# Scales of two attentions spread over partitions by transposes on TensorE instead of through a row in DRAM, and two matmul groups reordered by height

## Chip, core and metric

The kernel runs on one core of one Trainium2 chip. The metric is the device time of one execution in microseconds, the median of three runs.

## The reference, cut to what matters

The reference is one transformer block followed by a second block of two layers, on a sequence of 1024 tokens of width 1024, in float32. The first block mixes tokens by a chunked gated linear attention (4 heads) and by a causal attention with low-rank projections (MLA, 8 heads with values of 64 channels); a cross attention to 256 memory tokens and a feed-forward part with a short convolution follow. The second block has an even layer (a state-space scan beside a long convolution) and an odd layer, a differential attention of 8 heads with values of 128 channels:

```
MLA:   p = softmax(sc);  o = p @ v                        (8 heads, 64 channels)
odd:   wts = softmax(sc_0) - lam * softmax(sc_1);  o = wts @ v     (8 heads, 128 channels)
       o = rmsnorm(o, subln_w) * (1 - lam_init);  o = o * silu(gate);  out = x + o @ w_out
GLA:   o_intra + o_inter = (q k^T, masked) v + q S;   S <- decay * S + k^T v   (chunks of 64)
even:  decay = exp(where(tril, cs_l - cs_s, -inf)) for each head and chunk
```

In both attentions each query's output has one factor that is known only after its scores: the reciprocal of the softmax sum in the MLA attention, the reciprocal root of the mean square in the odd one.

## The kernel before

A sequence of stages, each with its own tile pools, goes over 8 tiles of 128 tokens. Matmuls work on split operands, a high and a low part, with three matmuls for each product (`mm3`, lines 263 to 265). PSUM has four buffers of 512 columns (`pa`) and two of 1024 (`pb`). The framework lays the instructions of each engine in one order when the program is built, by priority in the order of the code, with waits on semaphores between engines; `later` shifts the priority.

The frame of both attentions is `attend`. It walks over steps, each a head and a pair of query tiles `t0`, in the order 6, 4, 2, 0 (`ORDER`; the first MLA head the other way round). In a step it lays the scores of the next step, the transposes of this step's probabilities (`trans2`, line 773), the products with the values, and, through `pop`, some independent work from a queue: output projections, gate projections. A step ends with `finish`, which may return a function; that is called at the end of the next step, and what it returns again one step later. Four query tiles make a group `g` (0 or 1), two groups a head.

The outputs are held transposed: channels on partitions, tokens along the columns. The factors lie with tokens on partitions, one column for each tile. To multiply, the factors must stand along the columns on every partition:

- In the odd attention (`odd_attn`), `finish` makes `H.y`. `sums`, a step later, adds up the squares on TensorE and, with the second pair of a group, takes the root (`root`, lines 178 to 182: ten short VectorE instructions). It then writes the four columns as a row to DRAM (line 1633) and reads the row back to all 128 partitions (line 1635), both from SyncE's queue. `scale`, one step later again, multiplies on GpSimd (line 1617). Head 7's group 0 doesn't take this way: it is scaled at the output. When both groups of a head are scaled, `split_y` makes the high part on ScalarE (line 1679) and the low part on GpSimd (line 1680), and the output projections can use them.
- In the MLA attention (`mla`), two heads share a tile: 64 channels each. `norm` takes the reciprocal of four columns for each head (line 926), writes a row (line 928) and reads it to 64 partitions (line 931). After the odd head of a pair, `scale` multiplies on GpSimd (line 919), and the split into high and low follows on ScalarE and GpSimd (lines 920, 921). Heads 6 and 7 take another way for the first four tiles (`direct`).

Two other places are touched. In `gla`, `step` makes for each of four heads one matmul over 128 rows (line 624) and two over 64 rows (line 626) into one PSUM tile; each call of 128 columns stands as two instructions in the profile. In `even`, each of 4 heads in 8 turns takes one matmul of a selector column over 64 rows of `csT` (line 1291) and one of a mask over 128 rows (line 1292).

Of the kernel before, what the change touches and what calls it, by code (L numbers as in the profile page):

```python
# [19 lines left out]
P = 128  # L20
# [14 lines left out]
class Kern:  # L35
# [64 lines left out]
    def setup(self):  # L100
# [24 lines left out]
        self.sel = self.cpool_const([64, 16], F32R)  # L125
        nc.vector.tensor_tensor(self.sel, self.ident[:64, 0:16], self.ident[:64, 32:48], op=ALU.add)
# [447 lines left out]
    def gla(self, qT, ki, kt, E, vt, sg):  # L574
# [28 lines left out]
        def step(t):  # L603
# [16 lines left out]
            for hd in range(4):  # L620
                j, hh = hd // 2, hd % 2
                r = slice(hh * 64, hh * 64 + 64)
                ol = slice(hh * 512 + j * P, hh * 512 + j * P + P)
                mm(po[:, ol], at[t][:, hh * 2 + j], vt[t][:, hd * P:(hd + 1) * P], start=True, stop=False)
                for c in range(2):
                    mm(po[c * 64:(c + 1) * 64, ol], qT[j][r, t * P + c * 64:t * P + c * 64 + 64], S_in[c][j][r, :],
                       start=False, stop=True)
# [204 lines left out]
    def mla(self, h, qT, kT, v, side):  # L832
        nc, a = self.nc, self.a
        mm = nc.tensor.matmul
        pair, vhl, sums, rbs, raw = {}, {}, {}, {}, {}
# [19 lines left out]
        def scores(st, q):  # L855
# [14 lines left out]
            if hd not in sums:  # L870
                sums[hd] = self.small(8, tag="rsm", bufs=3)
            nm, rs = self.small(1, tag="nm", bufs=6), sums[hd][:, t:t + 1]
# [17 lines left out]
        def finish(step, po):  # L890
# [26 lines left out]
            def scale():  # L917
                gc = slice(g * 512, g * 512 + 512)
                nc.gpsimd.tensor_tensor(o, o, rbs[g], op=ALU.mult)
                nc.scalar.copy(oh[:, gc], o)  # L920
                nc.gpsimd.tensor_tensor(ol[:, gc], o, oh[:, gc].bitcast(F32), op=ALU.subtract)
                done(range(g * 4, g * 4 + 4))

            def norm():
                sg = sums[hd][:, g * 4:g * 4 + 4]
                nc.vector.reciprocal(sg, sg)
                row = self.dram.tile([4, P], F32, name="row1", tag="row1", bufs=4)
                nc.sync.dma_start(out=row.rearrange("t p -> p t"), in_=sg)
                if hd % 2 == 0:
                    rbs[g] = self.slot("rb", [P, 512])  # L930
                nc.sync.dma_start(out=rbs[g][r], in_=row.rearrange("t p -> (t p)").partition_broadcast(64))
                return scale if hd % 2 else None

            return norm
# [183 lines left out]
    def even(self, X, usum, rs, spill, zsp, ysp):  # L1118
# [72 lines left out]
        for g in range(4):  # L1191
# [52 lines left out]
            if g == 0:  # L1244
                csT = self.sb.tile([64, S], F32R, name="csT", tag="csT", bufs=1)
# [3 lines left out]
                nc.vector.tensor_scalar(csT, self.ident[:64, 0:1].to_broadcast([64, S]), 0.0, None, op0=ALU.mult)  # L1249
# [31 lines left out]
            for i in range(2):  # L1281
# [6 lines left out]
                for e in range(4):  # L1288
                    hd = 4 * g + e
                    ps = self.psum()  # L1290
                    mm(ps, self.sel[:, hd:hd + 1].to_broadcast([64, P]), csT[:, i * 512:(i + 1) * 512], start=True, stop=False)
# [220 lines left out]
    def odd_attn(self, X, h3, out, qs, ks, vs, gs):  # L1512
# [21 lines left out]
        def start(hd):  # L1534
# [12 lines left out]
            H.y, H.rb, H.yhl = None, {}, {}  # L1547
# [57 lines left out]
        def finish(st, po):  # L1605
# [8 lines left out]

            def scale():
                gc = slice(g * 512, g * 512 + 512)
                nc.gpsimd.tensor_tensor(H.y[:, gc], H.y[:, gc], H.rb[g], op=ALU.mult)
                H.scaled += 1

            def sums():  # L1620
# [6 lines left out]
                ts = self.last(t0)  # L1627
                if ts:
                    c = slice(ts[0], ts[0] + 4)
                    self.root(H.rstd[:, c], H.ss[:, c], self.small(4))  # L1630
                    if hd < 7 or g:
                        row = self.dram.tile([4, P], F32, name="row", tag="row", bufs=4)
                        nc.sync.dma_start(out=row.rearrange("t p -> p t"), in_=H.rstd[:, c])
                        H.rb[g] = self.slot("rb", [P, 512])
                        nc.sync.dma_start(out=H.rb[g], in_=row.rearrange("t p -> (t p)").partition_broadcast(P))
# [115 lines left out]
def body(tc, a, out, h_in=None, stages="ABCDE"):  # L1751
    with ExitStack() as ctx:
# [69 lines left out]
        if "E" in stages:  # L1822
# [13 lines left out]
            XO.enter_context(K.pool("oa", v=4, vu=2, vr=2, sg=2, pt=4, y=4, rb=2, gt=3, tmp=4))  # L1836
# [25 lines left out]
```

## Time and profile before

| | |
|---|---|
| median of 3 runs | 3262.02 us (3260.43 to 3266.59) |
| profiled execution | 3269.77 us; span 3267.8 us |
| mean granted clock of TensorE | 0.956 |
| linear attention, steps | about 220 to 282 us |
| MLA attention | about 385 to 625 us |
| even layer | about 1540 to 2290 us |
| odd attention | about 2780 to 3268 us |

Times in the profile are microseconds from the start of the span. PE is TensorE, PEld its loads of weights, DVE VectorE, ACT ScalarE, POOL GpSimd, SP SyncE. Busy time of an engine counts its instructions, not its waits. PEclk is the clock that TensorE was granted, as a share of full speed. A row of the windows view gives the stretch, its length, the busy time and count of instructions of PE, PEld, DVE, ACT and POOL, then PEclk, the share of time in which the DMA engines moved data, and GB/s. In a row of waits, the engine and line ahead of the arrow waited for what stands behind it.

### The profile page before, as it was taken

How to read it: one execution, taken by the hardware profiler on the slowest of the kernel's cores; microseconds unless marked ns; L12 is line 12 of the kernel's file. 1: busy time of each engine (PE TensorE's matmuls, PEld its weight loads, DVE VectorE, ACT ScalarE, POOL GpSimd, SP SyncE). 2: the span in 40 equal slices, each digit the busy share in tenths (PEclk: the TensorE clock that was granted, in tenths of full speed). 3: DMA queues.
4: the chain of work that ended last, by engine and by line, in shares of the span. 5: the costliest groups of instructions: out<-in, count | busy, mean ns of one | idle time of the engine just before them, and what ended most of it. 6: DMA issues, size and time to landing. Idle time of an engine off the chain costs nothing.

```text
span 3267.8 us, 38496 instructions
## 1 busy us (share of the span) xinstructions
PE 3020.2 (92%) x14638; PEld 2447.1 (75%) x14646; DVE 1930.5 (59%) x3114; ACT 1129.9 (35%) x2090; POOL 868.7 (27%) x776
## 2 busy tenths in 40 slices
PE   8999888889999999999999999999999999996777
PEld 7777666677788888888878777777777888784665
DVE  4324766765443334333898979785885550684555
ACT  4421554634311211121432323232334331553443
POOL 2111611112212221221134242434512220223434
PEclk9988989999999999999999999999999999997878
DMA  3011101110211111111211111123323562545321
GB/s 114 26 46 50 38 17 17 43 46 20 78 39 52 52 52 39 52 52 54 79 49 50 55 55 50 55 62 124 151 71 111 147 203 82 143 122 159 94 55 65
DMA packets 186156, 234.25 MB, mean 72 GB/s; under 512 B 31069, under 2 KB 121717, under 8 KB 185973
## 3 DMA queue, kind: packets, MB, share of 16 engines
q1 hardware_dynamic: 166901, 202.44, 20.9%
q10 hardware_dynamic: 15616, 16.78, 1.6%
q0 software_dynamic: 3456, 12.58, 1.0%
q8 instruction: 115, 1.88, 0.3%
q14 instruction: 68, 0.56, 0.1%
HBM read 181.37 MB, written 50.39 MB: 71 GB/s over the span
## 4 chain that ended last, share of the span: by engine, by line
PE 61%; DVE 14%; DMA 9%; issue 6%; POOL 4%; ACT 3%; SPq 0%; POOLq 0%; DVEq 0%; ACTq 0%
PE pa_t L263 9%; PE pa_t L264 9%; PE pa_t L265 9%; PE pb_t L265 8%; PE pb_t L264 8%; PE pb_t L263 8%; DMA row<-rsy_t 3%; DVE acc_t L1143 3%; DMA rb_t<-row 2%; PE pa_t L773 1%; PE pb_t L868 1%; DVE wl_t L202 1%; PE pa_t L887 1%; DVE h_t L290 1%; POOL wl_t L202 1%
## 5 line engine op out<-in xcount | busy, mean ns | idle before, releaser
L202 POOL TENSOR_TENSOR wl_t<-wr_t,wh_t 128x349 fp32r<-128x349 f32 (+2 forms) x221 | 294.9, 1337 | 1250.4 <-ACT wh_t L197 1208.7
L263 PE MATMUL pb_t<-x_t,wh_t 128*128 128x512 f32 x1312 | 518.5, 396 | 2.0 <-ACT wh_t L197 0.9
L265 PE MATMUL pb_t<-x_t,wl_t 128*128 128x512 f32 x1312 | 515.7, 393 | 0.9 <-DVE wl_t L202 0.9
L264 PE MATMUL pb_t<-x_t,wh_t 128*128 128x512 f32 x1280 | 505.3, 395 | 0.1
L197 ACT CAST wh_t<-wr_t 128x1024 fp32r<-128x1024 f32 (+2 forms) x221 | 217.4, 993 | 552.8 <-PE pb_t L264 256.2
L202 DVE TENSOR_TENSOR wl_t<-wr_t,wh_t 128x675 fp32r<-128x675 f32 (+1 forms) x195 | 207.8, 1070 | 305.4 <-ACT wh_t L197 304.9
L263 PE MATMUL pa_t<-wh_t,x_t 128*128 128x512 f32 (+3 forms) x1024 | 374.3, 366 | 2.6 <-ACT wh_t L197 0.8
L264 PE MATMUL pa_t<-wl_t,x_t 128*128 128x512 f32 (+3 forms) x1024 | 371.3, 363 | 0.5 <-DVE wl_t L202 0.3
L1143 DVE SCALAR_TENSOR_TENSOR acc_t<-u_t,c,acc_t 128x1024 f32<-128x1024 f32 x240 | 339.3, 1416 | 2.9
L290 DVE TENSOR_TENSOR h_t<-h_t,pa_t 128x512 f32<-128x512 f32 x336 | 226.5, 685 | 150.6 <-PE pa_t L265 148.7
L263 PEld LDWEIGHTS pb_t<-x_t,wh_t 128*128 128x128 f32 x1312 | 247.4, 189 | 57.1 <-ACT wh_t L197 1.8
L265 PEld LDWEIGHTS pb_t<-x_t,wl_t 128*128 128x128 f32 x1312 | 247.3, 188 | 55.6 <-DVE wl_t L202 2.1
L264 PEld LDWEIGHTS pb_t<-x_t,wh_t 128*128 128x128 f32 x1280 | 241.4, 189 | 52.9 <-DVE x_t L212 1.0
L265 PE MATMUL pa_t<-wh_t,x_t 128*128 128x512 f32 (+3 forms) x640 | 221.3, 346 | 0.0
L263 PEld LDWEIGHTS pa_t<-wh_t,x_t 128*128 128x128 f32 x1024 | 192.4, 188 | 33.7 <-ACT wh_t L197 2.0
L265 PE MATMUL pa_t<-wh_t,xl_t 128*128 128x512 f32 x512 | 205.6, 402 | 11.6 <-POOL xl_t L1680 11.6
L264 PEld LDWEIGHTS pa_t<-wl_t,x_t 128*128 128x128 f32 x1024 | 192.5, 188 | 30.9 <-DVE wl_t L202 2.1
L209 DVE TENSOR_TENSOR pt_t<-pa_t,pt_t 128x512 fp32r<-128x512 f32 (+2 forms) x240 | 120.0, 508 | 99.0 <-ACT pt_t L208 97.4
L263 PE MATMUL pa_t<-wh_t,g_t 128*128 128x512 f32 x384 | 150.2, 391 | 3.2 <-DVE h_t L290 1.4
L264 PE MATMUL pa_t<-wl_t,g_t 128*128 128x512 f32 x384 | 149.5, 389 | 0.0
L265 PE MATMUL pa_t<-wh_t,g_t 128*128 128x512 f32 x352 | 136.8, 389 | 1.1 <-POOL g_t L340 1.1
L208 ACT CAST pt_t<-pa_t 128x512 fp32r<-128x512 f32 (+2 forms) x240 | 105.5, 443 | 78.1 <-PE pa_t L773 49.5
(501 smaller groups left out, 5983.8 us busy)
## 6 DMA issues: line engine op xcount, KB each, us to landing
wr_t<-in_a_w_in SPq DMA_DIRECT2D x46, 512.0 KB
wr_t<-in_c_w_in SPq DMA_DIRECT2D x26, 512.0 KB
wr_t<-in_ffn_w_gate SPq DMA_DIRECT2D x22, 512.0 KB
wr_t<-in_ffn_w_up SPq DMA_DIRECT2D x22, 512.0 KB
wr_t<-in_ffn_w_down SPq DMA_DIRECT2D x22, 512.0 KB
h_t<-in_x SPq DMA_DIRECT2D x16, 512.0 KB
wr_t<-in_a_w_out SPq DMA_DIRECT2D x16, 512.0 KB
lo_t<-ks SPq DMA_DIRECT2D x64, 128.0 KB
```

The costliest lines, as they stand in the source:

```text
L197: nc.scalar.copy(hi, raw)
L202: e.tensor_tensor(*[x[:, c] for x in f], op=ALU.subtract)
L208: nc.scalar.copy(hi, src)
L209: nc.vector.tensor_tensor(lo, src, hi.bitcast(F32), op=ALU.subtract)
L263: mm(out, lh, rh, start=st, stop=False)
L264: mm(out, lh, rl, start=False, stop=False)
L265: mm(out, ll, rh, start=False, stop=en)
L290: self.nc.vector.tensor_tensor(h[t][:, c], h[t][:, c], ps, op=ALU.add)
L773: self.nc.tensor.transpose(pt[:, i * 256 + q * P:i * 256 + (q + 1) * P], w[t0 + q][:, (b0 + i) * P:(b0 + i + 1) * P], self.ident)
L868: mm(sp[:, c0:c0 + wd], qT[:96, hd, t * P:(t + 1) * P], kT[:96, hd, c0:c0 + wd], start=True, stop=c0 + wd < n)
L887: mm(po[:, q:256], vhl[hd][:, kb], x[:, i * 256 + q:i * 256 + 256], start=kb == 0 and j == 0, stop=kb == t0 + 1 and j == 1)
L1143: nc.vector.scalar_tensor_tensor(acc, u[:, k:k + S], cw31(k, c), acc, op0=ALU.mult, op1=ALU.add)
```

## The change

In both attentions the row in DRAM goes. In the odd one, `scale` transposes each of the four columns, broadcast to 128 columns, on TensorE into one PSUM tile of 128x512, and VectorE multiplies `H.y` by it. In the MLA attention the sums of a pair of heads share a tile of 16 columns; `norm` runs once for a pair and takes the reciprocal of the sums broadcast over 64 channels, 512 columns in all; `scale` transposes four blocks of 128 columns into PSUM, and VectorE multiplies. In `gla` the four matmuls over 128 rows come first and then the sixteen instructions over 64 rows, with one start for each PSUM bank. In `even`, selector and `csT` have 128 rows, the added ones zero.

```diff
--- before.py
+++ after.py
@@ -122,8 +122,8 @@
         nc.gpsimd.memset(self.maskT4, 0.0)
         nc.gpsimd.affine_select(out=self.maskT4, in_=self.maskT4, compare_op=ALU.is_ge, fill=NEG, base=0,
                                 pattern=[[0, 4], [1, P]], channel_multiplier=-1)
-        self.sel = self.cpool_const([64, 16], F32R)
-        nc.vector.tensor_tensor(self.sel, self.ident[:64, 0:16], self.ident[:64, 32:48], op=ALU.add)
+        self.sel = self.cpool_const([P, 16], F32R)
+        nc.vector.tensor_tensor(self.sel, self.ident[:, 0:16], self.ident[:, 32:48], op=ALU.add)
         self.identb = self.cpool_const([P, P], BF16)
         nc.vector.tensor_copy(self.identb, self.ident)
         self.causal = self.cpool_const([P, P], BF16)
@@ -617,14 +617,15 @@
                                                    op0=ALU.mult, op1=ALU.add)
                     st[j] = new
             po = self.psum("pb")
-            for hd in range(4):
-                j, hh = hd // 2, hd % 2
-                r = slice(hh * 64, hh * 64 + 64)
-                ol = slice(hh * 512 + j * P, hh * 512 + j * P + P)
-                mm(po[:, ol], at[t][:, hh * 2 + j], vt[t][:, hd * P:(hd + 1) * P], start=True, stop=False)
-                for c in range(2):
-                    mm(po[c * 64:(c + 1) * 64, ol], qT[j][r, t * P + c * 64:t * P + c * 64 + 64], S_in[c][j][r, :],
-                       start=False, stop=True)
+            heads = [(hd, hd // 2, hd % 2) for hd in range(4)]
+            ol = lambda j, hh: slice(hh * 512 + j * P, hh * 512 + j * P + P)
+            for hd, j, hh in heads:
+                mm(po[:, ol(j, hh)], at[t][:, hh * 2 + j], vt[t][:, hd * P:(hd + 1) * P], start=j == 0, stop=False)
+            for c in range(2):
+                for hd, j, hh in heads:
+                    r = slice(hh * 64, hh * 64 + 64)
+                    mm(po[c * 64:(c + 1) * 64, ol(j, hh)], qT[j][r, t * P + c * 64:t * P + c * 64 + 64], S_in[c][j][r, :],
+                       start=False, stop=j == 1)
             po = po.rearrange("p (b r) -> p b r", b=2)[:, :, 0:256].rearrange("p b (j v) -> p j b v", j=2)
             if t % 2 == 0:
                 o = self.slot("x", [P, 2, 512])
@@ -832,7 +833,7 @@
     def mla(self, h, qT, kT, v, side):
         nc, a = self.nc, self.a
         mm = nc.tensor.matmul
-        pair, vhl, sums, rbs, raw = {}, {}, {}, {}, {}
+        pair, vhl, sums, inv, raw = {}, {}, {}, {}, {}
 
 
         def direct(hd, t):
@@ -867,9 +868,9 @@
                 wd = min(512, n - c0)
                 mm(sp[:, c0:c0 + wd], qT[:96, hd, t * P:(t + 1) * P], kT[:96, hd, c0:c0 + wd], start=True, stop=c0 + wd < n)
             mm(sp[:, t * P:n], self.identb, self.causal, start=False, stop=True)
-            if hd not in sums:
-                sums[hd] = self.small(8, tag="rsm", bufs=3)
-            nm, rs = self.small(1, tag="nm", bufs=6), sums[hd][:, t:t + 1]
+            if hd // 2 not in sums:
+                sums[hd // 2] = self.small(16, tag="rsm", bufs=3)
+            nm, rs = self.small(1, tag="nm", bufs=6), sums[hd // 2][:, hd % 2 * 8 + t:hd % 2 * 8 + t + 1]
             nc.vector.tensor_reduce(nm, sp[:, :n], axis=AX.X, op=ALU.max, negate=True)
             p = self.slot("p", [P, S])
             nc.scalar.activation(p[:, :n], sp[:, :n], AF.Exp, bias=nm, accum_out=rs)
@@ -916,22 +917,22 @@
 
             def scale():
                 gc = slice(g * 512, g * 512 + 512)
-                nc.gpsimd.tensor_tensor(o, o, rbs[g], op=ALU.mult)
+                rb = self.psum()
+                for j in range(4):
+                    nc.tensor.transpose(rb[:, j * P:(j + 1) * P], inv[g][:, j * P:(j + 1) * P], self.ident)
+                nc.vector.tensor_tensor(o, o, rb, op=ALU.mult)
                 nc.scalar.copy(oh[:, gc], o)
                 nc.gpsimd.tensor_tensor(ol[:, gc], o, oh[:, gc].bitcast(F32), op=ALU.subtract)
                 done(range(g * 4, g * 4 + 4))
 
             def norm():
-                sg = sums[hd][:, g * 4:g * 4 + 4]
-                nc.vector.reciprocal(sg, sg)
-                row = self.dram.tile([4, P], F32, name="row1", tag="row1", bufs=4)
-                nc.sync.dma_start(out=row.rearrange("t p -> p t"), in_=sg)
-                if hd % 2 == 0:
-                    rbs[g] = self.slot("rb", [P, 512])
-                nc.sync.dma_start(out=rbs[g][r], in_=row.rearrange("t p -> (t p)").partition_broadcast(64))
-                return scale if hd % 2 else None
-
-            return norm
+                sm = sums[hd // 2].rearrange("p (h t) -> p t h", h=2)[:, g * 4:g * 4 + 4]
+                inv[g] = self.slot("rb", [P, 512])
+                nc.vector.reciprocal(inv[g].rearrange("p (t h c) -> p t h c", t=4, h=2),
+                                     sm.unsqueeze(3).to_broadcast([P, 4, 2, 64]))
+                return scale
+
+            return norm if hd % 2 else None
 
         out = []
         st = {}
@@ -1242,11 +1243,11 @@
             x0 = xbc(wx, 0, 2 * g)
             x1 = xbc(wx, P, 2 * g + 1)
             if g == 0:
-                csT = self.sb.tile([64, S], F32R, name="csT", tag="csT", bufs=1)
+                csT = self.sb.tile([P, S], F32R, name="csT", tag="csT", bufs=1)
                 pc = self.psum("pb")
                 for t in range(NT):
                     tr(pc[:16, t * P:(t + 1) * P], cs[:, t], self.ident)
-                nc.vector.tensor_scalar(csT, self.ident[:64, 0:1].to_broadcast([64, S]), 0.0, None, op0=ALU.mult)
+                nc.vector.tensor_scalar(csT, self.ident[:, 0:1].to_broadcast([P, S]), 0.0, None, op0=ALU.mult)
                 nc.scalar.copy(csT[:16, :], pc[:16, :])
                 nc.vector.tensor_tensor(csT[32:48, :], pc[:16, :], csT[:16, :].bitcast(F32), op=ALU.subtract)
                 nc.vector.tensor_scalar(fl(cs), fl(cs), -1.0, None, op0=ALU.mult)
@@ -1288,7 +1289,7 @@
                 for e in range(4):
                     hd = 4 * g + e
                     ps = self.psum()
-                    mm(ps, self.sel[:, hd:hd + 1].to_broadcast([64, P]), csT[:, i * 512:(i + 1) * 512], start=True, stop=False)
+                    mm(ps, self.sel[:, hd:hd + 1].to_broadcast([P, P]), csT[:, i * 512:(i + 1) * 512], start=True, stop=False)
                     mm(ps, self.identb, self.maskT4, start=False, stop=True)
                     M = self.slot("MT", [P, 512])
                     for m in range(4):
@@ -1544,7 +1545,7 @@
                             nc.sync.dma_start(out=x[o:o + 64], in_=ks[hd, i, m * 64:m * 64 + 64, c])
                     H.q[g, m], H.k[g, m], H.kl[g, m] = (x.bitcast(F32R) for x in (q, k, kl))
             H.rstd, H.s0, H.ss = (self.small(8, tag="rsy", bufs=9) for _ in range(3))
-            H.y, H.rb, H.yhl = None, {}, {}
+            H.y, H.yhl = None, {}
             H.scaled = 0
 
         def values(hd):
@@ -1612,9 +1613,14 @@
                 H.y = self.slot("y", [P, S])
             nc.vector.scalar_tensor_tensor(H.y[:, c], po[:, 0:256], ycol, H.sg[g][:, t0 % 4 * P:t0 % 4 * P + 256], op0=ALU.mult, op1=ALU.mult)
 
+            ts = self.last(t0)
+
             def scale():
                 gc = slice(g * 512, g * 512 + 512)
-                nc.gpsimd.tensor_tensor(H.y[:, gc], H.y[:, gc], H.rb[g], op=ALU.mult)
+                rb = self.psum()
+                for j, t in enumerate(ts):
+                    tr(rb[:, j * P:(j + 1) * P], H.rstd[:, t:t + 1].to_broadcast([P, P]), self.ident)
+                nc.vector.tensor_tensor(H.y[:, gc], H.y[:, gc], rb, op=ALU.mult)
                 H.scaled += 1
 
             def sums():
@@ -1624,15 +1630,10 @@
                 e = self.small(2, tag="se", bufs=4)
                 nc.scalar.activation(e, H.s0[:, c], AF.Square, scale=EPS ** 0.5)
                 nc.vector.scalar_tensor_tensor(H.ss[:, c], po[:, 256:258], 1.0 / P, e, op0=ALU.mult, op1=ALU.add)
-                ts = self.last(t0)
                 if ts:
                     c = slice(ts[0], ts[0] + 4)
                     self.root(H.rstd[:, c], H.ss[:, c], self.small(4))
                     if hd < 7 or g:
-                        row = self.dram.tile([4, P], F32, name="row", tag="row", bufs=4)
-                        nc.sync.dma_start(out=row.rearrange("t p -> p t"), in_=H.rstd[:, c])
-                        H.rb[g] = self.slot("rb", [P, 512])
-                        nc.sync.dma_start(out=H.rb[g], in_=row.rearrange("t p -> (t p)").partition_broadcast(P))
                         return scale
 
             return sums
@@ -1833,7 +1834,7 @@
                 with K.pool("op", tok=2, ev=4, v=2, sg=2, tmp=3):
                     K.odd_proj(X, qs, ks, vs, gs, cs2)
             XO.enter_context(K.pool("w3", wr=2, wh=4, wl=4))
-            XO.enter_context(K.pool("oa", v=4, vu=2, vr=2, sg=2, pt=4, y=4, rb=2, gt=3, tmp=4))
+            XO.enter_context(K.pool("oa", v=4, vu=2, vr=2, sg=2, pt=4, y=4, gt=3, tmp=4))
             XO.enter_context(K.pool("oe", "right", e=4))
             K.odd_attn(X, h3, out, qs, ks, vs, gs)
             XO.close()
```

## Rows read from the trace of the kernel before

**Rows 1.** Page: busy time by engine, the chain by line, one costly group.

```profile
PE 3020.2 (92%) x14638; PEld 2447.1 (75%) x14646; DVE 1930.5 (59%) x3114; ACT 1129.9 (35%) x2090; POOL 868.7 (27%) x776
...
PE pa_t L263 9%; PE pa_t L264 9%; PE pa_t L265 9%; PE pb_t L265 8%; PE pb_t L264 8%; PE pb_t L263 8%; DMA row<-rsy_t 3%; DVE acc_t L1143 3%; DMA rb_t<-row 2%; PE pa_t L773 1%; PE pb_t L868 1%; DVE wl_t L202 1%; PE pa_t L887 1%; DVE h_t L290 1%; POOL wl_t L202 1%
...
L290 DVE TENSOR_TENSOR h_t<-h_t,pa_t 128x512 f32<-128x512 f32 x336 | 226.5, 685 | 150.6 <-PE pa_t L265 148.7
```

**Rows 2.** Busy time by stretch of the odd attention (windows view).

```profile
2831.00:2930.00 99.00, 95.83 (x575) 79.43 (x575) 81.64 (x189) 57.74 (x147) 21.38 (x15) 0.98 0.53 131
2930.00:3234.00 304.00, 221.69 (x1167) 181.51 (x1166) 173.71 (x387) 130.86 (x332) 116.16 (x87) 0.84 0.34 89
3234.00:3268.00 34.00, 25.01 (x85) 18.95 (x85) 11.34 (x25) 6.45 (x11) 11.64 (x9) 0.80 0.35 131
```

**Rows 3.** Timeline of SyncE's queue, odd attention: start us, us, what.

```profile
2952.70 0.53 SPq L1633 DMA_DIRECT2D row<-rsy_t  x1
2960.97 0.33 SPq L1635 DMA_DIRECT2D rb_t<-row  x1
```

**Rows 4.** Timeline of ScalarE in the same turn.

```profile
2950.67 0.22 ACT L1625 ACTIVATE se_t<-rsy_t 128x2 f32<-128x2 f32 x1
2967.19 0.62 ACT L1679 CAST xl_t<-y_t 128x512 fp32r<-128x512 f32 x1 [16.30 <-POOL y_t L1617]
```

**Rows 5.** Waits from 2940 to 3268 us: us in total, times, longest.

```profile
ACT xl_t L1679 <- POOL y_t L1617: 93.5, 11, 16.3
```

**Rows 6.** Busy time by stretch of the MLA attention (windows view).

```profile
424.00:457.00 33.00, 20.53 (x104) 14.41 (x103) 13.85 (x26) 14.00 (x35) 6.34 (x5) 0.82 0.07 13
457.00:484.00 27.00, 26.40 (x142) 20.16 (x140) 19.32 (x38) 14.28 (x37) 1.28 (x1) 0.91 0.04 6
...
576.00:600.00 24.00, 24.00 (x133) 18.03 (x133) 20.22 (x43) 16.30 (x41) 1.62 (x1) 0.96 0.03 6
600.00:625.00 25.00, 19.59 (x92) 14.64 (x92) 15.55 (x35) 12.28 (x31) 4.39 (x4) 0.86 0.24 69
sum 225.00, PE 187.47 PEld 137.92 DVE 146.05 ACT 119.77 POOL 32.41; mean PE 23.43 PEld 17.24 DVE 18.26 ACT 14.97 POOL 4.05
```

**Rows 7.** Waits from 380 to 640 us.

```profile
ACT o_t L920 <- POOL or_t L919: 40.0, 7, 8.3
```

**Rows 8.** Timeline of TensorE around one group of four transposes.

```profile
2857.66 0.60 PE L773 MATMUL pa_t<-c,e_t 128*128 128x128 f32 x4
...
2858.02 0.48 PE L1582 MATMUL pb_t<-lo_t 128*128 128x512 f32 x1
```

**Rows 9.** Timeline of VectorE, one root: its first and last of ten.

```profile
2856.90 0.16 DVE L178 TENSOR_SCALAR rsy_t<-rsy_t 128x4 int32<-128x4 int32 x1
...
2862.74 0.16 DVE L182 SCALAR_TENSOR_TENSOR rsy_t<-sm_t,rsy_t 128x4 f32<-128x4 f32 x1
```

**Rows 10.** Reciprocals of lines 926 and 1108: ns min/median/max, shape.

```profile
L926 DVE RECIPROCAL rsm_t<-rsm_t x14: 165/168/178, 401.1 to 599.9; 128x4 f32<-128x4 f32 x14
...
L1108 DVE RECIPROCAL MT_t<-MT_t x1: 939/939/939, 1622.8 to 1622.8; 128x128 f32<-128x128 f32 x1
```

**Rows 11.** Chain that ended last, linear attention: start us, us, what.

```profile
242.09 1.07 PE pa_t L611 x16
243.17 0.72 PE pb_t L624 x2
243.89 0.62 PE pb_t L626 x4
```

**Rows 12.** Busy time in the linear attention (windows view).

```profile
228.00:265.00 37.00, 36.76 (x228) 23.36 (x230) 15.05 (x44) 6.01 (x10) 4.90 (x3) 0.50 0.12 36
```

**Rows 13.** Chain that ended last, even layer.

```profile
1872.80 0.42 PE pa_t L1291
1873.22 0.32 PE pa_t L1292
...
1874.75 0.23 PE pb_t L263
```

## Prediction

> **What bounds the kernel now.** I read the page first. TensorE is busy for 92% of the span, and the chain of work that ended last is mostly its matmuls; but two transfers through the DRAM row stand in that chain by name, 3% and 2% of 3267.8 us, about 160 us [rows 1]. Next I cut the odd attention into stretches. From 2831 to 2930 us TensorE is busy 95.83 of 99 us at a granted clock of 0.98; from 2930 to 3234 it is busy 221.69 of 304 us at 0.84 [rows 2]. Both run the same loop, so the second shows what the first would lose to a wait. The timeline of one turn tells which. SyncE issues the row at 2952.70 and reads it back at 2960.97 [rows 3]; GpSimd then multiplies, and ScalarE, which finished its last short instruction at 2950.89, stands until 2967.19 for that product [rows 4]. ScalarE does its instructions in the order laid down, and the exponentials of the next scores are behind that cast; TensorE runs out of work and then comes back at the lower of its two clock levels (1.2 instead of 2.4 GHz), which is why the mean falls. The waits view counts it: ScalarE stood 93.5 us in 11 pieces for the product [rows 5]. In the first 99 us the same trips happen, but no cast of y stands on ScalarE yet: the reader should see that the trip alone costs nothing.
>
> The MLA attention has the same picture, in four stretches (424 to 457, 484 to 516, 541 to 576, 600 to 625 us; the first and last are shown) of 125 us with 455 matmuls. The three full stretches between them (first and last shown) hold 405 matmuls in 76 us [rows 6]. ScalarE waited 40.0 us for the product there [rows 7].
>
> **Odd attention: what goes.** 15 pairs of DMAs and 15 GpSimd multiplies. One trip, from the row's issue at 2952.70 to the cast's start at 2967.19, is 14.5 us [rows 3, 4]. What comes is four transposes on TensorE and one VectorE product that reads PSUM. Four transposes of 128x128 hold TensorE 0.36 us, start to next start (2857.66 to 2858.02) [rows 8]. The product I price by the add of a 128x512 PSUM tile, 0.685 us [rows 1]. With a hop between engines the new trip is between 1.1 us and, if it queues behind a reduction on VectorE, some 3 us.
>
> How much of the 304 us goes? By TensorE: 575 matmuls took 99 us, 0.172 us each, so the 1167 need 201 us, plus 11 groups of transposes at 0.36, 4 us: 205 us. By VectorE: its work there is 173.71 us [rows 2], plus 11 products, 7.5 us, gives 181.2 us; in the full stretch its share was 81.64/99 = 0.825, and at that share 181.2 us take 220 us. I take 220, the later of the two: **84 us saved**. Bounds: 99 (TensorE alone) and about 42 (half of the wait stays). In the last 34 us TensorE is idle for 9 us and at 0.80 clock [rows 2]; part of that is the last trip, while eight output tiles of head 7 cover the rest: **5 us**, between 0 and 9.
>
> The removed GpSimd multiply covers nothing else. SyncE's queue, which held the loads of the next head behind each row, gets free earlier; those loads wait for slots that TensorE frees, so I count nothing, and no loss either, since nothing is moved ahead of them. The transposes take one of four PSUM buffers of the "pa" kind until VectorE has multiplied; score transposes and output tiles use the same four. Price: nothing while VectorE follows within the 3 us above, up to 3 us x 15 = 45 us if TensorE stops each time. That bound is inside the half case below.
>
> Where the change adds a wait: the transposes need the root of the norm, a chain of ten short VectorE instructions that lay 6.0 us apart from first to last [rows 9], and every matmul behind them on TensorE would wait. The code lays them one attention step after the root; the 99 us of the full stretch run from the first row issue of head 0 to that of head 2, two heads of four steps, so a step is about 12 us. So I take zero.
>
> **MLA attention.** 14 pairs of DMAs and 7 GpSimd multiplies go. Seven groups of transposes (0.36 us) and seven products (0.685) come, and the 14 reciprocals of 4 columns become 7 of 512 columns, since the broadcast over channels is done before the reciprocal. That is the cost: 128x4 takes 0.168 us and 128x128 takes 0.939 [rows 10], so 6.22 ns a column, and 512 columns take 0.168 + 508 x 6.22 ns = 3.33 us. VectorE gains 7 x (3.33 + 0.685) - 14 x 0.168 = 25.8 us. Everything behind a reciprocal on VectorE waits: the row maxima, then ScalarE's exponentials, then TensorE.
>
> By TensorE the four stalled stretches would take 455 x 76/405 = 85.4 instead of 125 us: 39.6 saved at most. By VectorE: 146.05 + 25.8 = 171.8 us, at its highest share in a full stretch, 20.22/24 = 0.84 [rows 6], take 204 us instead of 225: **21 us saved**. Lower bound: the 25.8 us fully exposed, 14 us.
>
> The 3.33 us is extended from the shape nearest in size, a quarter as wide. The Trainium skill, "VectorE: DVE Perf Modes", section "First, the fixed hardware budget", says that a reciprocal runs as an iterative divide with a repeat count of 8; with the 0.96 GHz of its specifications I estimate from that page 8.3 ns a column, 4.3 us for 512. By the row the sum is the one below; by the page it would be 7 x 0.95/0.84, some 8 us later. The slope of the two rows, 6.22 ns, does not bear the 8 cycles out, so the row's price stands.
>
> **The reordering.** In the gated linear attention a step alternates full-height matmuls (line 624) with 64-row ones (line 626), four times. At half clock a pair of the first holds the chain 0.72 us and four of the second 0.62; sixteen 64-row matmuls in a row (line 611) take only 1.07, 0.067 each [rows 11]. So four should take 0.27, and 0.35 us is the change of shape. I take the same 0.35 off a pair that follows its own kind (no row shows it; bounds 0 and 0.35). Six of eight changes go: 6 x 0.35 = 2.1 us a step, and TensorE is busy 36.76 of 37 us here at 0.50 clock [rows 12], so it counts in full: seven steps, **15 us**. Bounds: 7, and 34 if the clock rises to the upper level too (a step of 7.6 us would be 5.5 at half clock and 2.8 at full).
>
> In the even layer a 64-row matmul (line 1291) and a full-height one (1292) alternate 32 times: 0.42 + 0.32 us in the chain, where equal-height 512-column matmuls follow each other in 0.23 [rows 13]. With 128 rows for both, 0.74 becomes 0.46, 32 x 0.28 = 9 us. VectorE's convolutions end some of those waits; I take **7 us**, bounds 0 and 9. The larger zero fill is one instruction.
>
> **Sum.** 84 + 5 + 21 + 15 + 7 = 132 us. The profiled execution took 3269.77 us, 2 us outside its span; minus 132 gives 3138. It lies 7.75 us above the median of the three runs, 3262.02, so for the median **3130 us**. Own range of this case: 3095 to 3165.
>
> **Rivals.**
> Half of the wait stays: ScalarE's cast still stands ahead of the exponentials and waits for a product that queues on VectorE behind reductions, reciprocals and root. For it: VectorE is at 0.82 already. Against: the new trip is 1 to 3 us, not 14.5. Saved (84 + 21)/2 + 27 = 79 us: 3182 us.
>
> TensorE becomes the only bound, VectorE fills up past 0.84, and the clock of the linear attention rises: odd 99, MLA 39, GLA 34, the rest 12, 184 us: 3078 us. Against: no stretch shows it.
>
> Slower: the wait moves onto TensorE. The 22 groups of transposes stand in TensorE's queue and hold everything behind them until the scales are ready. If the planner puts the odd ones straight behind their root they wait 6.0 us each, 90 us, and the MLA ones for a reciprocal, 23 us: 113 us, about what the trips cost (110), and the clock falls after each stop, for which I add 40 us from the present mean of 0.84. 3262 - 22 + 3 + 40 = 3283 us. It decides from some 5 us of wait per group. Against: the step of 12 us between root and transposes.
>
> No change: the trips' time hides, ScalarE then waits as long for something else, and the reciprocals eat the reordering's 22 us. Only rows of full idle behind the product speak against it, but they are clear: about 3262.
>
> **Chances.** Forecast 0.58, half case 0.25, TensorE-bound 0.10, slower 0.05, no change 0.02. The range reaches from the TensorE-bound case to past the half case: 3080 to 3200. A change under 0.2% (6.5 us) can't be told from none. Faster 0.93, same 0.02, slower 0.05.
>
> **What would show it.** Right: no row of DRAM in the chain; ScalarE's wait for the product under 30 us; TensorE over 90% busy and the clock over 0.92 in the odd attention after its first two heads; the MLA reciprocals near 3.3 us each; lines 1291 and 1292 about 0.23 us apart; a GLA step of 5.5 us. Wrong: a wait of TensorE for the root or for inv, VectorE over 0.9 busy with TensorE idle, or ScalarE still standing at the casts of lines 920 and 1679.

## The result, and the profile after

The changed kernel takes 3118.36 us (median of 4 runs, 3115.11 to 3120.15) beside 3264.31 us of the kernel before on the same chip (4 runs): ratio 0.9553, interval 0.9536 to 0.9569, 146 us faster. The forecast was 3130 us in a range of 3080 to 3200, and faster. The profiled execution took 3115.11 us with a span of 3113.4, against 3267.8: 154.4 us less. The mean granted clock is 0.984, against 0.956.

The page, with busy time by engine, the chain by engine and the chain by line:

```profile
PE 2959.9 (95%) x14726; PEld 2413.3 (78%) x14734; DVE 1958.0 (63%) x3129; ACT 1128.7 (36%) x2090; POOL 839.4 (27%) x754
...
PE 68%; DVE 14%; issue 5%; POOL 4%; DMA 3%; ACT 3%; SPq 0%; POOLq 0%; DVEq 0%; ACTq 0%
PE pa_t L263 11%; PE pa_t L264 11%; PE pa_t L265 11%; PE pb_t L265 8%; PE pb_t L264 8%; PE pb_t L263 8%; DVE acc_t L1144 3%; PE pa_t L774 2%; PE pb_t L869 1%; DVE wl_t L202 1%; PE pa_t L888 1%; PE pb_t L1583 1%; DVE h_t L290 1%; DMA wr_t<-in_c_w_in 1%; PE pb_t L1584 1%
```

Both rows of DRAM have left the chain [rows 1], and TensorE is the only large item in it. TensorE's own busy time fell by 60 us although 88 records more are listed: its instructions are shorter where the clock is at the upper level.

Windows of the changed kernel, in this order: linear attention, MLA attention, odd attention from its third head on, the end:

```profile
226.00:240.00 14.00, 13.72 (x220) 10.86 (x219) 11.28 (x37) 5.04 (x9) 0.00 (x0) 1.00 0.28 78
356.00:560.00 204.00, 192.15 (x1064) 139.62 (x1063) 179.06 (x322) 128.94 (x316) 27.37 (x23) 0.98 0.05 16
2864.00:3086.00 222.00, 205.43 (x1225) 170.56 (x1224) 182.16 (x404) 132.92 (x335) 101.16 (x76) 0.98 0.34 104
3086.00:3113.00 27.00, 20.45 (x88) 15.78 (x86) 10.78 (x24) 7.07 (x12) 11.56 (x9) 0.94 0.41 156
```

The third row answers to the 304 us at clock 0.84 in [rows 2]: the same heads take 222 us at 0.98. The second answers to the stretches of [rows 6]: the mean clock is 0.98, where two of those shown stood at 0.82 and 0.86. The first answers to [rows 12]: the clock went from 0.50 to 1.00. The last is 27 us where there were 34.

Waits from 350 to 565 us, the MLA attention (us in total, times, longest):

```profile
ACT o_t L924 <- DVE or_t L923: 1.3, 2, 0.8
```

ScalarE's wait for the product there, 40.0 us before [rows 7], is down to 1.3.

Waits from 2864 to 3086 us (us in total, times, longest):

```profile
ACT xl_t L1680 <- DVE y_t L1623: 4.0, 3, 1.7
...
PE pa_t L1622 <- DVE rsy_t L1632: 2.6, 1, 2.6
```

The wait of 93.5 us [rows 5] is down to 4.0 us. The second row is the wait of which the rival on the slower side was made: TensorE stood ahead of the transposes for a norm, once, for 2.6 us.

One new trip in the timeline, TensorE's four transposes and VectorE's product:

```profile
2882.11 0.60 PE L1622 MATMUL pa_t<-c,rsy_t 128*128 128x128 f32 x4
...
2882.75 0.69 DVE L1623 TENSOR_TENSOR y_t<-y_t,pa_t 128x512 f32<-128x512 f32 x1 [0.88 <-PE pa_t L1622]
```

From the first weight load at 2881.88 to the end of the product at 2883.44 are 1.6 us; the way through DRAM took 14.5, to the start of the cast [rows 3, 4].

Where the 154 us are, by the first and last starts of each stage's lines: the odd attention 451.8 to 370.1 us, its last output tiles 7 us less; MLA attention 235.6 to 203.7; linear attention 132.6 to 105.4; even layer 573.7 to 571.4. Together some 150 us. Of the 154 us the medians show 146: the profiled execution before lay 5.5 us above its median, the one after 3.3 us below.

### The profile page after: what moved, and what is told of

Its sections match the earlier page's. It is cut to its first block, busy times and chain, and to the rows that moved or that the text cites. A ratio compares the mean times of both kernels' runs of the same rounds, so it can differ in the third digit from the quotient of the medians.

```text
span 3113.4 us, 38565 instructions
## 1 busy us (share of the span) xinstructions
PE 2959.9 (95%) x14726; PEld 2413.3 (78%) x14734; DVE 1958.0 (63%) x3129; ACT 1128.7 (36%) x2090; POOL 839.4 (27%) x754
## 4 chain that ended last, share of the span: by engine, by line
PE 68%; DVE 14%; issue 5%; POOL 4%; DMA 3%; ACT 3%; SPq 0%; POOLq 0%; DVEq 0%; ACTq 0%
PE pa_t L263 11%; PE pa_t L264 11%; PE pa_t L265 11%; PE pb_t L265 8%; PE pb_t L264 8%; PE pb_t L263 8%; DVE acc_t L1144 3%; PE pa_t L774 2%; PE pb_t L869 1%; DVE wl_t L202 1%; PE pa_t L888 1%; PE pb_t L1583 1%; DVE h_t L290 1%; DMA wr_t<-in_c_w_in 1%; PE pb_t L1584 1%
```

## Experiments

The kernel before was timed again beside the experiments, on two chips, here called A and B: 3278.41 and 3277.09 us on A, 3277.0 us on B, 13 to 14 us above the 3264.31 us of the result. The changed kernel came to 3118.71 us on B, within 0.4 us of its result. So its ratio was 0.951 there and 0.9553 in the result, and experiments are compared by their ratios or by stage lengths. The traces from A say where those us are: in kernels with one part of the change the untouched stages took 455 to 457 us (odd attention), 240 to 241 (MLA), 134 (linear) and 575 to 577 (even layer), together some 14 us more than in the trace of the kernel before. Why is open.

### Each part alone

Four kernels, all run on A, carry one part of the diff each: the odd attention's scale, the MLA attention's, the order in `gla`, or the 128 rows in `even`. The lines that matter, the rest cut:

```diff
 odd_only:
-                nc.gpsimd.tensor_tensor(H.y[:, gc], H.y[:, gc], H.rb[g], op=ALU.mult)
+                    tr(rb[:, j * P:(j + 1) * P], H.rstd[:, t:t + 1].to_broadcast([P, P]), self.ident)
+                nc.vector.tensor_tensor(H.y[:, gc], H.y[:, gc], rb, op=ALU.mult)
 mla_only:
-                nc.gpsimd.tensor_tensor(o, o, rbs[g], op=ALU.mult)
+                    nc.tensor.transpose(rb[:, j * P:(j + 1) * P], inv[g][:, j * P:(j + 1) * P], self.ident)
+                nc.vector.tensor_tensor(o, o, rb, op=ALU.mult)
 gla_only:
-            for hd in range(4):                (one full-height, then its 64-row ones)
+            for hd, j, hh in heads:            (all full-height)
+            for c in range(2):                 (then all 64-row ones)
 even_only:
-                    mm(ps, self.sel[:, hd:hd + 1].to_broadcast([64, P]), ...)
+                    mm(ps, self.sel[:, hd:hd + 1].to_broadcast([P, P]), ...)
```

> The kernel before with the odd attention's part of the change alone. Theory (the stages add, each gains by its own wait): the odd attention gained 88 us between the two traces (81.7 to the last matmul of line 1622, 6.6 behind it), so 3264 - 88 = 3176 us, ratio 0.973, and ScalarE's wait at the cast of y below 20 us instead of 93.5. Rival (the gain came in part from the earlier stages, since an earlier or denser start shifts the loads of this one): at most 70 us, 3194 us or more.

> The kernel before with the MLA attention's part alone, the reciprocals of 512 columns included. Theory (stages add): the MLA attention gained 32 us between the two traces, so 3232 us, ratio 0.990. Rival (VectorE's 25.8 us of added work bind, as the prediction's term of 21 us had it, and the rest came with the shift from the linear attention): 21 us, 3243 us, ratio 0.9935.

> The kernel before with the linear attention's reordering alone. Theory (fewer changes of shape also bring the clock to its upper level, as in the trace after, where the stage stands at 1.00): 27 us, 3237 us, ratio 0.9917, granted clock about 1.0 between 220 and 255 us. Rival (six changes of shape at the lower clock, as the prediction took it; the clock came from something else in the change): 15 us, 3249 us, ratio 0.9954, clock 0.5.

> The kernel before with 128 rows for the selector and for csT in the even layer alone. Theory (the pairs take 0.46 us instead of 0.74, but VectorE's convolutions end the waits around them, so the saved 9 us of TensorE come back as waits): 0 to 3 us, ratio between 0.999 and 1.000. Rival (TensorE's chain counts, as the prediction had it): 7 us, ratio 0.998.

| part alone | median us | ratio, interval | by the ratio | stage length: before, part alone, whole change |
|---|---|---|---|---|
| odd_only | 3188.01 | 0.9734 (0.9714 to 0.9755) | 87 us | 451.8, 372.4, 370.1 |
| mla_only | 3245.72 | 0.9905 (0.9884 to 0.9927) | 31 us | 235.6, 204.1, 203.7 |
| gla_only | 3254.08 | 0.9934 (0.9916 to 0.9952) | 22 us | 132.6, 105.6, 105.4 |
| even_only | 3275.57 | 0.9990 (0.9974 to 1.0005) | 3 us | 573.7, 570.2, 571.4 |

The column before is from the trace of the kernel before, not from A. By the stages the parts add: each stage is as long with its part alone as with all four, within 2.3 us. By the ratios they make 143 us, with some 12 us either way from the four intervals. The result's 146 us lies inside; the 158 us of the changed kernel on B do not quite, so a rest of some us that only the whole change has is not excluded.

The odd and the MLA part came out as the theory had it; the MLA part's rival, ratio 0.9935, lies outside the interval. The linear part's time lies between its two cases, 0.9917 and 0.9954, but its stage is shorter by 27 us and its clock is at the upper level, as the theory had it. The even part can't be told from none by its time, and its interval holds the rival's 0.998 too. The even layer's length wanders by some us from kernel to kernel, so the means say more: 574.8 us in the six traces without this part, 570.6 in the eight with it, 4.2 us, between the two cases.

In odd_only the wait at the cast is 4.0 us as in the whole change. In gla_only the window of the steps shows that the reordering alone brings the clock up:

```profile
226.00:240.00 14.00, 13.72 (x215) 10.90 (x218) 11.28 (x38) 4.87 (x8) 0.00 (x0) 1.00 0.25 77
```

### Is it the trip, or what stands behind it?

Two kernels keep the row in DRAM and its 14.5 us and move only the point at which `scale` is laid. odd_late returns it one step later in the code. odd_dep does that as well, and makes the product depend on a sum of the newest scores by way of a tiny VectorE and a tiny GpSimd instruction, so that the planner must place the cast later too. `heads["new"]` is the newest of those sums. The lines that matter:

```diff
 odd_late, in sums:
-                        return scale
+                        return lambda: scale
 odd_dep, the same, and in scale, ahead of the multiply:
+                one = self.small(1, tag="one", bufs=4)
+                nc.vector.tensor_scalar(one, heads["new"], 0.0, 1.0, op0=ALU.mult, op1=ALU.add)
+                nc.gpsimd.tensor_tensor(H.rb[g][:, 0:1], H.rb[g][:, 0:1], one, op=ALU.mult)
```

> The kernel before, the row in DRAM and the GpSimd multiply kept, but the multiply of the odd attention is laid one attention step (about 12 us) later, and with it everything that follows from it. Theory (a trip of 14.5 us costs only because ScalarE's cast stands behind it in a fixed order; laid later, the cast finds its product ready): ScalarE's wait at the cast falls from 93.5 us below 40, and 50 to 80 us are saved, 3185 to 3215 us. Rival (the trip itself, or GpSimd's 1.26 us product, is what limits): the same wait comes back one step later, under 20 us saved.

Measured: 3280.97 us, ratio 1.0004 (0.9988 to 1.0019), no change, against my expectation. Waits of odd_late from 2940 to 3278 us:

```profile
ACT xl_t L1679 <- POOL y_t L1617: 100.8, 10, 17.6
```

The wait is still there. The order of ScalarE's instructions says why: a line that is laid later in the code was placed nearly where it had been, so odd_late did not move what it was to move, and tests nothing. Number of exponentials (line 1593 of the kernel before) ahead of each of the 16 casts of y on ScalarE, counted in the traces:

```
before    60 60 60 60 62 64 67 74 83 92  99 108 114 120 128 128
odd_late  60 60 60 60 62 64 67 74 83 92  99 108 114 122 128 128
odd_only  60 60 60 60 62 64 68 76 84 92 100 108 116 124 128 128
odd_dep   60 60 60 60 62 64 72 80 88 96 104 112 119 128 128 128
```

> As odd_late, the row in DRAM kept, but here GpSimd's multiply reads in addition a one made from the newest softmax sum, so that the order itself must place product and cast later: each cast of y now stands behind five more exponentials on ScalarE than before (72, 80, 88, 96 exponentials ahead of the casts instead of 67, 74, 83, 92; in odd_late they were the same 67, 74, 83, 92). Theory (the trip costs only because the fixed order lays the cast where the planner thinks the row is back): ScalarE's wait at the casts falls from about 95 us below 40, and 40 to 80 us are saved, 3195 to 3235 us at a before of 3275. Rival (the trip's length costs wherever the cast stands, because the output tiles need it): the wait moves to TensorE at the low parts, under 20 us saved.

Measured: 3214.16 us, ratio 0.9806 (0.9792 to 0.9821), 64 us faster with the row kept. Waits of odd_dep from 2940 to 3212 us:

```profile
ACT xl_t L1683 <- POOL y_t L1621: 24.1, 9, 7.4
```

The window of odd_dep from the third head on:

```profile
2940.00:3186.00 246.00, 210.04 (x1152) 170.83 (x1150) 181.18 (x391) 129.37 (x326) 111.70 (x94) 0.92 0.46 105
```

In odd_dep the casts of the middle heads moved behind 4 to 8 more exponentials; the wait fell from 100.8 to 24.1 us, the stretch from 304 to 246 us and the whole stage from 451.8 to 390 us. In odd_only they stand nearly where they stood, at most 4 exponentials later, and there the short trip took the wait to 4.0 us. So the wait needs two things, a long trip and exponentials that are laid behind a cast which needs its end. Taking away the first saved 87 us; taking away the second, with the trip kept, saved 64, some three quarters of that. That the planner takes the trip for shorter than it is, is inferred from these places and was not seen directly.

### Does the engine of the product matter?

odd_pool (on A) keeps the transposes, copies their PSUM tile to SBUF on VectorE and multiplies on GpSimd, as before the change.

```diff
-                nc.vector.tensor_tensor(H.y[:, gc], H.y[:, gc], rb, op=ALU.mult)
+                rs = self.slot("rb", [P, 512])
+                nc.vector.tensor_copy(rs, rb)
+                nc.gpsimd.tensor_tensor(H.y[:, gc], H.y[:, gc], rs, op=ALU.mult)
```

> The changed kernel, but in the odd attention VectorE copies the transposed scales from PSUM to SBUF and GpSimd multiplies again: the trip through DRAM is gone, GpSimd keeps its 1.26 us product and VectorE is as busy as in the changed kernel. Theory (the length of the trip decides, 14.5 us against some 3): within 10 us of the changed kernel, 3118 to 3128 us. Rival (moving the product from GpSimd to VectorE is a good part of the gain): 3140 us or more.

Measured: 3128.48 us, ratio 0.9548 (0.9532 to 0.9564), within 0.4% of the changed kernel's 0.951 on B. It is 9.5 us over gla_half, a kernel below that ran on A too and takes as long as the changed one; the theory allowed 10. Waits from 2864 to 3120 us:

```profile
ACT xl_t L1682 <- POOL y_t L1625: 15.8, 8, 3.4
```

The wait grows by 12 us and the stage from 370.1 to 379.0, a tenth of what the change took off it. With the casts where they are, the length of the trip is what counts; GpSimd's multiply was a small part of it.

### What do the wide reciprocals cost?

mla_narrow takes the reciprocal of the 8 sums and then copies it out over 512 columns; narrow_pool has the copy on GpSimd. mla_double makes the wide reciprocal twice, which adds its cost once more. The lines that matter:

```diff
 mla_narrow:
-                nc.vector.reciprocal(inv[g]..., sm.unsqueeze(3).to_broadcast([P, 4, 2, 64]))
+                nc.vector.reciprocal(sm, sm)
+                nc.vector.tensor_copy(inv[g]..., sm.unsqueeze(3).to_broadcast([P, 4, 2, 64]))
 narrow_pool, in place of the second of these:
+                nc.gpsimd.tensor_copy(inv[g]..., sm.unsqueeze(3).to_broadcast([P, 4, 2, 64]))
 mla_double:
                 nc.vector.reciprocal(inv[g]..., sm.unsqueeze(3).to_broadcast([P, 4, 2, 64]))
+                nc.vector.reciprocal(inv[g]..., sm.unsqueeze(3).to_broadcast([P, 4, 2, 64]))
```

> The changed kernel, but in the MLA attention the reciprocal is taken of the eight sums, 0.17 us, and a VectorE copy spreads them over 512 columns (some 0.5 us) in place of the 3.34 us reciprocal: 7 x 2.7 = 19 us less on VectorE. Theory (VectorE is not what ends the MLA stage, TensorE is; it was above the share of 0.84 that the prediction took as its limit): 0 to 6 us under the changed kernel, 3112 to 3118 us, ratio 0.9535 to 0.9553. Rival (VectorE binds as the prediction's sum has it): 15 to 19 us, about 3101 us, ratio 0.950.

> The changed kernel with each 512-column reciprocal of the MLA attention done twice, 7 x 3.34 = 23.4 us more on VectorE. Theory (VectorE limits the MLA stage in part: taking 19 us away shortened it by 13 to 14 us): the stage, 203.7 us from its first scores to its last product with the values, grows by 15 to 23 us. Rival (the reciprocals are hidden and the narrow kernel gained by a better order): under 8 us.

> The changed kernel with the reciprocal of the eight sums and with the spreading copy on GpSimd instead of VectorE, 7 x 0.43 us less on VectorE than in mla_narrow. Theory (VectorE limits the MLA stage in part): 2 us under mla_narrow, ratio 0.946 to 0.947, some 0.8% under the changed kernel of the same call. Rival (GpSimd's copy is late, its queue holds the low parts, and the transposes wait on TensorE): 5 us or more over mla_narrow, ratio 0.949.

| kernel | chip | median us | ratio, interval | MLA stage us |
|---|---|---|---|---|
| changed kernel again | B | 3118.71 | 0.9510 (0.9493 to 0.9527) | 204.2 |
| mla_double | B | 3135.70 | 0.9560 (0.9544 to 0.9577) | 219.9 |
| mla_narrow | A | 3101.86 | 0.9469 (0.9456 to 0.9482) | 189.8 |
| narrow_pool | B | 3107.27 | 0.9478 (0.9464 to 0.9492) | 190.1 |

> The changed kernel once more, unchanged, beside the others of this call: ratio 0.955, with 0.953 to 0.957 as before. It is the yardstick for the next one.

The ratio is 0.951 and not the expected 0.955; the changed kernel's own time is the same within 0.4 us, and it is the kernel before that was slower on B.

The reciprocals of the changed kernel by line, ns min/median/max:

```profile
L931 DVE RECIPROCAL rb_t<-rsm_t x7: 3341/3343/3347, 394.7 to 541.3; 128x512 f32<-128x512 f32 x7
```

The same lines of mla_narrow, the reciprocal and the copy:

```profile
L931 DVE RECIPROCAL rsm_t<-rsm_t x7: 192/195/207, 397.2 to 532.7; 128x8 f32<-128x8 f32 x7
L932 DVE COPY rb_t<-rsm_t x7: 417/427/428, 397.5 to 533.3; 128x512 f32<-128x512 f32 x7
```

The window of the MLA stage in mla_narrow:

```profile
358.50:548.30 189.80, 183.65 (x1063) 136.10 (x1062) 160.62 (x329) 129.28 (x315) 28.04 (x22) 1.00 0.05 18
```

And in mla_double:

```profile
358.30:578.20 219.90, 197.31 (x1059) 142.00 (x1058) 199.99 (x327) 127.11 (x312) 25.54 (x20) 0.96 0.05 15
```

0.62 us take the place of 3.34, seven times. VectorE's busy time falls by 18.4 us and the stage by 14.2; doubled, it rises by 20.9 and the stage by 15.9. Some three quarters of what is added to VectorE or taken from it reaches the end of the stage, in both directions. So mla_narrow went against its theory, by which VectorE does not end this stage, and for its rival. With the narrow form TensorE is busy 183.65 of 189.8 us at clock 1.00, and I take it for the bound. narrow_pool, which takes the copy off VectorE as well, agrees with that: its stage is no shorter, and neither the 2 us of its theory nor the 5 us of its rival showed. mla_narrow is the best version here: 0.5% under the kernel of the next experiment, which ran on A too, has the wide reciprocals and takes as long as the changed kernel (0.9515); their intervals don't meet.

### How many changes of height may stay?

gla_half reorders within pairs of heads: two heads' full-height matmuls, then their 64-row ones, twice, so that four changes of height stay in a step instead of two. The lines that matter, without the loop over the 64-row ones:

```diff
-            for hd, j, hh in heads:            (all four)
+            for pr in (heads[:2], heads[2:]):
+                for hd, j, hh in pr:           (full height, then the 64-row ones of the pair)
```

> The changed kernel with the linear attention's matmuls ordered by pairs of heads: two full-height, eight 64-row instructions, and again, so four changes of shape a step instead of two (before: eight). Theory (the clock's level makes the larger part; with four changes TensorE still stands near the upper level): 3 to 8 us over the changed kernel, 3121 to 3126 us, clock near 1.0 in the stage. Rival (with four changes the clock falls to the lower level as before): about 18 us over it, 3136 us, clock near 0.5.

Measured: 3119.0 us, ratio 0.9515 (0.9498 to 0.9532), the same as the changed kernel; the 3 to 8 us that I expected on top don't show. Its window shows the upper level too, with TensorE busy all the time:

```profile
226.00:240.00 14.00, 14.00 (x204) 10.20 (x203) 10.55 (x37) 4.86 (x8) 0.00 (x0) 1.00 0.24 77
```

Two windows of the kernel before, as its clock falls:

```profile
225.00:226.00 1.00, 1.00 (x11) 0.66 (x10) 0.89 (x3) 0.00 (x0) 1.00 (x1) 1.00 0.00 0
227.00:228.00 1.00, 1.00 (x17) 0.67 (x14) 0.39 (x2) 0.57 (x1) 0.00 (x0) 0.50 0.00 0
```

A window of narrow_pool, which has the changed order:

```profile
228.00:236.00 8.00, 8.00 (x97) 6.31 (x95) 3.34 (x10) 2.30 (x4) 0.00 (x0) 0.67 0.21 67
```

In all six traces with eight changes a step the clock falls to 0.50 in the first steps and is 0.50 from 228 to 270 us. With fewer changes it did not always stay at 1.00: in four of the seven traces with two changes (odd_pool, narrow_pool, mla_narrow, and the changed kernel run again) it fell once or twice for a few us, but rose again inside the stage. The stage took 110.1 us in narrow_pool, with two falls, against 105.4 with none. The one trace with four changes has no fall.

Rows of the chain that ended last, the kernel before just as its clock falls (line 624 is full height, 626 has 64 rows):

```profile
225.49 0.42 PE pb_t L624 x2
225.91 0.36 PE pb_t L626 x4
226.27 0.59 PE pb_t L596 x2
226.87 1.07 PE pa_t L611 x16
227.94 0.72 PE pb_t L624 x2
```

The chain of gla_half, where these are lines 624 and 628:

```profile
228.94 0.64 PE pb_t L624 x4
229.59 0.38 PE pb_t L628 x8
```

The chain of the changed kernel, lines 623 and 627:

```profile
231.44 1.09 PE pb_t L623 x8
232.52 0.68 PE pb_t L627 x16
```

At the upper level a quarter of the work took 0.42 + 0.36 = 0.78 us one head at a time, half of it 0.64 + 0.38 = 1.02, all of it 1.09 + 0.68 = 1.77. So 3.12, 2.04 and 1.77 us a step with eight, four and two changes of height: about 0.14 us for each of the last two, 0.27 for each of the four before. From eight changes to two that is 1.35 us a step, over seven steps an estimated 9 us of the 27. The larger part of the gain is the second thing in the first chain: line 611, untouched, takes 1.07 us once the clock is down and 0.61 after the change. gla_half has the changed kernel's start flags as well as its own order, two starts in a step where the kernel before has four; order and starts were not tested apart.

## Why the prediction was right, point by point

**Odd attention, 84 us: right in mechanism and size.** The stretch was to become 220 us and is 222; VectorE's work there was put at 181.2 us and is 182.16, the product at 0.685 us and is 0.69. The matmuls and the clock (0.98) came back as in the first two heads. What the prediction said, that ScalarE had exponentials laid behind a cast that needs the trip's end, odd_dep bears out, with 64 us saved and the trip kept; odd_only bears out that a short trip is enough, with the casts nearly in place. In odd_late a later place in the code did not move the cast. That VectorE sets the 222 us, as I took it, agrees with the number but was not tested apart: TensorE is busy 205.43 of them.

**The end, 5 us:** 7 by the windows, 34 to 27.

**MLA attention, 21 us: too small, 32.** The reciprocal's price was right, 3.33 us against 3.343. The estimate of 4.3 us, worked out from the repeat count of 8 that the Trainium skill, "VectorE: DVE Perf Modes", section "First, the fixed hardware budget", states, is not borne out by this shape. The failed step is "at its highest share in a full stretch, 0.84": VectorE's 179.06 us would take 213 by that share and took 204. Its share is 0.88 here and 0.91 in mla_double, so 0.84 was no limit but what that stretch happened to need. Of the work added to VectorE about three quarters counted. By mla_narrow the stage is some 190 us without the wide reciprocals, 46 less than in the trace before; the wide form gives 14 of these back.

**Linear attention, 15 us: too small, 27.** I took six changes of height at 0.35 us and let the clock stand at 0.50. It went to 1.00 and a step from 7.6 to 3.1 us (1.09 + 0.68 + 0.70 + 0.61 in the chain, and short gaps), not to 5.5. In the prediction this was the upper bound of 34 us and a part of the rival in which TensorE becomes the only bound. The Trainium skill, "TensorEngine Tiling (Array Packing)", section "Key Properties", says that a change of tiling mode drains TensorE; the chains agree, at 0.14 to 0.27 us a change at the upper level. That the alternation also goes with the lower level is what these runs add: with eight changes a step the clock fell in the first steps and stayed down to near the end of the stage in all six traces; with four or two it was at 1.00 but for a few us in some. Why the chip lowers it there is not shown.

**Even layer, 7 us: too large, about 4.** The pair did become 0.46 us, but VectorE's convolutions end waits around it, as in this chain of the changed kernel:

```profile
1802.21 1.23 DVE g_t L1187
...
1808.09 0.23 PE pa_t L1292
1808.33 0.23 PE pa_t L1293
```

**The sum:** 132 us against 154 between the two profiled executions. MLA and linear attention, some 23 us above their terms together, make the difference. The forecast of 3130 stood only 12 us above the median, since by the medians the gain is 146 us and not 154.

**The rivals.** Half of the wait stays (3182): no, 4 of 93.5 us. TensorE the only bound (3078): its clock part came true; VectorE went past 0.84 in the MLA stage and not in the odd attention, 0.82. Slower, with the wait on TensorE (3283): 2.6 us at the longest from 2864 to 3086, so the step between root and transposes was cover enough. No change: no.

## What to carry to other kernels

Where an engine works in order, look at what is laid behind the instruction that waits: a trip of 14.5 us cost nothing in one part of the loop and 87 us in the rest; shorten the trip, or give the planner a dependency that puts the waiting instruction later, since moving the line in the code may move nothing. Take a reciprocal on the few numbers and spread it by a copy: 0.62 us for 3.34. Lay matmuls of one height together, and read the granted clock of the stretch before pricing a reordering, since the clock can be the larger part.

## What the runs showed of the hardware that was not expected

- Full-height and 64-row matmuls in turn, eight changes a step, went with a granted clock of 0.50 to near the end of the stage in six of six traces. With four or two changes and the same work it was 1.00 in four of eight traces, and in the other four but for one or two falls of a few us.
- A share of 0.84 of one engine in a stretch without waits was no ceiling: 0.88 and 0.91 were reached when it was given more to do.
- The mean granted clock of the MLA stage was 0.96, 0.98 and 1.00 with two wide reciprocals for each group, with one and with none.
